# One index matmul for two parts of h: queries of tokens 64 to 255, and h's parts interleaved token by token

## The chip, the cores and the metric

The kernel runs on one core of a Trainium2 chip. The metric is the device time of one execution in microseconds (us); lower is better. TensorE (PE) multiplies, ScalarE (ACT), VectorE (DVE) and GpSimd (POOL) do the elementwise work, and SyncE (SP) issues all transfers, in order.

## The reference

One hybrid layer on x of 256 tokens by 4096. A vector c gives shift, scale and gate through w_ada (4096 x 12288); h, the modulated RMS norm of x, goes through one projection w_in, whose columns are split over a gated MLP, an attention and the attention's indexer.

```
mod = jax.nn.silu(c) @ w_ada + b_ada
shift, scale, gate = jnp.split(mod, 3, axis=-1)
h = rms_norm(x, norm_g) * (1 + scale) + shift          # (1, 256, 4096)
z = h @ w_in
uA, vA, gA, qB, kB, vB, gB, qI, kI, wI = jnp.split(z, offs, axis=-1)
yA = chunked_sgu(uA, vA, ...)
dots  = einsum('bqhd,bsd->bqhs', qI, kI)               # 32 index heads of 128
score = einsum('bqh,bqhs->bqs', wI, relu(dots))
score = where(causal, score, -inf)
_, sel = lax.top_k(score, 64)                          # 64 keys for each query
yB = attention of q over the selected keys and values, with a bias by distance
y  = concat([norm(yA) * silu(gA), norm(yB) * silu(gB)]) @ w_out
out = x + gate * y
```

A token t has t + 1 causal keys. For the tokens 0 to 63 these are at most 64, so top_k takes all of them whatever the scores are.

## The kernel before

All matmuls of the projections run in a 32-bit form with reduced precision (F32R), and float32 accuracy comes from splitting both operands in two: h = h_hi + h_lo, w = w_hi + w_lo, and the product is h_hi w_hi + h_lo w_hi + h_hi w_lo. h is the stationary operand (128 rows of the contraction by 128 tokens), w the moving one (up to 512 columns), so a pair of one contraction row block and one column group takes 3 parts x 2 token blocks = 6 matmuls.

A *tile* is two contraction row blocks of one column group. `stream` lists the tiles in order, and `step(t)` does for each: `load_w(t + 3)` (SP, into one of 4 raw buffers), `split(t)` (ACT makes whi; DVE and POOL share wlo = raw - whi by columns, POOL taking 352 of 512 on average in the early part), the adds of a visit that ended two tiles earlier (`add_to`: DVE adds PSUM to the group's sum, in the first block ACT copies), one `tick` of the work that runs beside, and `multiply(t)`, 12 matmuls. whi and wlo have 4 buffers each, two tiles' worth.

The contraction (32 row blocks) is cut into 8 *blocks* of 4, since h of a block needs shift and scale of its rows, and these come from 16.8 MB of w_ada a block. While block b is multiplied, `pace` spreads the ada work of the next block over the tiles, 33 steps a block: a transfer of 512 KB (SP, 2 buffers), and DVE's multiply-add into `acc` (L196). A buffer comes free when DVE is done with it, and SP issues the next ada transfer and the raw loads behind it in that order. `make_h` then sums `acc` over partitions on PE (L265), scales on ACT, and subtracts on POOL and DVE.

Each block visits 23 column groups, two tiles each: first the index columns (32 heads of 128 and the 160 columns kw of index keys and head weights, cut into two visits of 336 columns and seven of 512), then v and u of the MLP, then q, k, v of the attention. That makes 4 tiles of 336 columns and 42 of 512. In block 7 there are no ada steps of h left; `indexer` runs beside it: for each of 8 groups of 4 heads and each token block n, `turn` transposes the queries on PE with the flip matrix (L531), ACT copies them, `weigh` multiplies with the keys (L547), ACT takes relu, and DVE adds with the head's weight. After the 8 blocks come the gate columns (128 tiles, contraction whole) and w_out (128 tiles, y as the stationary operand), with attention, mixing and the gate's ada work beside.

Of the kernel before, what the change touches and what calls it, by code (L numbers as in the profile page):

```python
# [15 lines left out]
P = 128  # L16
# [26 lines left out]
def layer(ctx, tc, x, c, w_ada, b_ada, norm_g, w_in, ln_v_g, ln_v_b, w_s, b_s, q_norm_g,  # L43
# [213 lines left out]
    h_hi, h_lo = {}, {}  # L257
# [57 lines left out]
    def make_h(b, accs):  # L315
# [9 lines left out]
        hh = hp.tile([P, nk, 256], F32R, name=f"hh{k0}")  # L325
        hts, hl = [], None
        for j in range(0, nk, 2):
            modulate(b, md, j, hh[:, j:j + 2])
            yield
# [51 lines left out]
    def visit(src, parts, ks, c0, w, read, soon=False, before=None):  # L381
        v = dict(src=src, parts=parts, ks=ks, c0=c0, w=w, read=read, soon=soon, before=before)
# [36 lines left out]
    def multiply(t):  # L419
# [5 lines left out]
        (ah, al), w, n_k = v["parts"], v["w"], len(v["ks"])  # L425
        nk = len(hi)
        todo = [(part, kk, n) for kk in range(nk) for part in range(2) for n in range(NT)]
        todo += [(2, kk, n) for kk in range(nk) for n in range(NT)]
        if t + 1 == len(stream):
            todo.sort(key=lambda x: x[2])  # L430
        for part, kk, n in todo:
            k = v["ks"][i + kk]
            a = al if part == 1 else ah
            b = lo if part == 2 else hi
# [642 lines left out]
```

## Time and profile before

| | us |
|---|---|
| median of 3 runs | 1894.25 (1889.58 to 1897.37) |
| the profiled execution | 1888.63 |
| its span, first to last instruction | 1886.9 |
| first matmul with h | 70.3 |
| blocks 0 to 7 of the contraction | 70.3 to 1120.8 |
| gate columns and w_out | 1120.8 to 1886.9 |

Times in rows are us from the span's start unless marked ns. PE's busy time includes the modelled ends of pipelined matmuls, so the distance from one start to the next tells its pace. A block's bounds are the starts of its first matmul: 70.3, 202.6, 328.3, 455.6, 581.8, 709.2, 836.1, 961.4, and 1120.8 for the gate columns.

### The profile page before, as it was taken

What the parts mean: (1) busy time and instruction counts of PE and PEld (TensorE: products, weight loads), DVE (VectorE), ACT (ScalarE), POOL (GpSimd) and SP (SyncE); (2) the same over time, 40 slices, a digit from 0 to 9 for tenths busy, and PEclk for the clock granted to TensorE, in tenths of its full rate; (3) what the DMA queues carried; (4) which work ended last, traced back from release to release, by engine and by line L of the source; (5) the groups of instructions that cost most, each with busy time, mean ns of one, the idle gap of its engine ahead of it and who ended that gap; (6) DMA issues with size and microseconds to landing.
All of it is one profiled execution on the core that took longest, in us unless ns stands there. A gap on an engine that the chain in (4) does not pass through costs nothing. (4 is left out here: it accounts for less than half of the span.)

```text
span 1886.9 us, 27998 instructions
## 1 busy us (share of the span) xinstructions
PE 1824.8 (97%) x8324; PEld 1490.3 (79%) x8324; DVE 1447.4 (77%) x1762; ACT 933.8 (49%) x1737; POOL 1295.3 (69%) x1339
## 2 busy tenths in 40 slices
PE   5799999999999999999999999999999999999998
PEld 2487878878888888788888777787888888888887
DVE  4666888888888888888777898877777677677754
ACT  4356545344453454444445556566654554444443
POOL 0366777777777777777675546766567777877786
PEclk9899999999999999999999999999999999999999
DMA  9999998999989989999874477876789799899964
GB/s 311 339 338 340 332 322 304 331 316 306 335 304 322 321 300 324 328 309 340 284 207 146 128 224 262 272 257 202 242 281 312 248 323 338 295 307 350 334 212 156
DMA packets 269554, 542.58 MB, mean 288 GB/s; under 512 B 17270, under 2 KB 29784, under 8 KB 269404
## 3 DMA queue, kind: packets, MB, share of 16 engines
q1 hardware_dynamic: 269404, 540.79, 84.6%
q8 instruction: 68, 1.11, 0.2%
q14 instruction: 82, 0.67, 0.1%
HBM read 536.51 MB, written 4.22 MB: 287 GB/s over the span
## 5 line engine op out<-in xcount | busy, mean ns | idle before, releaser
L416 POOL TENSOR_TENSOR wlo<-raw,whi 128x512 fp32r<-128x512 f32 (+1 forms) x1248 | 1220.3, 1004 | 536.9 <-ACT whi L408 448.2
L408 ACT ACTIVATE whi<-raw 128x512 fp32r<-128x512 f32 (+1 forms) x1248 | 730.9, 619 | 834.9 <-DMA raw<-in_w_in_dram 407.5
L414 DVE TENSOR_TENSOR wlo<-raw,whi 128x320 fp32r<-128x320 f32 (+2 forms) x624 | 640.7, 1028 | 323.2 <-ACT whi L408 209.4
L435 PE MATMUL mm_ps<-whi,hh 128*128 128x512 f32 (+1 forms) x1984 | 620.4, 394 | 11.4 <-ACT whi L408 9.4
L435 PE MATMUL mm_ps<-whi,hl 128*128 128x512 f32 (+1 forms) x1984 | 604.9, 386 | 2.4 <-DVE hl L303 2.4
L435 PE MATMUL mm_ps<-wlo,hh 128*128 128x512 f32 (+1 forms) x1984 | 525.4, 386 | 5.7 <-DVE wlo L414 4.1
L196 DVE SCALAR_TENSOR_TENSOR acc<-wa,csil,acc 128x1024 f32<-128x1024 f32 x341 | 436.3, 1279 | 57.1 <-DMA wa<-in_w_ada_dram 56.4
L435 PEld LDWEIGHTS mm_ps<-wlo,hh 128*128 128x128 f32 x1984 | 368.9, 188 | 83.8 <-POOL wlo L416 8.8
L435 PEld LDWEIGHTS mm_ps<-whi,hh 128*128 128x128 f32 x1984 | 363.5, 189 | 90.2 <-ACT whi L408 19.9
L435 PEld LDWEIGHTS mm_ps<-whi,hl 128*128 128x128 f32 x1984 | 371.2, 188 | 77.3 <-DVE hl L303 2.9
L435 PE MATMUL mm_ps<-whi,yh 128*128 128x512 f32 x512 | 158.2, 390 | 0.0
L435 PE MATMUL mm_ps<-whi,yl 128*128 128x512 f32 x512 | 158.0, 389 | 0.0
L435 PE MATMUL mm_ps<-wlo,yh 128*128 128x512 f32 x512 | 137.5, 390 | 0.2
L435 PEld LDWEIGHTS mm_ps<-wlo,yh 128*128 128x128 f32 x512 | 95.9, 188 | 21.2 <-POOL wlo L416 1.5
L435 PEld LDWEIGHTS mm_ps<-whi,yh 128*128 128x128 f32 x512 | 95.9, 188 | 20.4 <-ACT whi L408 0.4
L435 PEld LDWEIGHTS mm_ps<-whi,yl 128*128 128x128 f32 x512 | 96.1, 188 | 20.0
L802 DVE TENSOR_TENSOR qi<-qi,mm_ps 128x512 f32<-128x512 f32 (+2 forms) x126 | 73.2, 616 | 0.0
L217 PE MATMUL acc<-wa,csil 128*1 128x512 f32 x64 | 28.1, 629 | 13.2 <-DMA wa<-in_w_ada_dram 13.2
L802 DVE TENSOR_TENSOR u<-u,mm_ps 128x512 f32<-128x512 f32 x56 | 35.6, 675 | 0.0
L802 DVE TENSOR_TENSOR v<-v,mm_ps 128x512 f32<-128x512 f32 x56 | 35.6, 675 | 0.0
L802 DVE TENSOR_TENSOR q<-q,mm_ps 128x512 f32<-128x512 f32 x56 | 35.6, 675 | 0.0
L222 DVE SCALAR_TENSOR_TENSOR accs<-wa,csil,accs 128x1024 f32<-128x1024 f32 x15 | 19.2, 1283 | 17.9 <-DMA wa<-in_w_ada_dram 17.8
(173 smaller groups left out, 797.2 us busy)
## 6 DMA issues: line engine op xcount, KB each, us to landing
raw<-in_w_in_dram SPq DMA_DIRECT2D x464, 512.0 KB, 5.9
wa<-in_w_ada_dram SPq DMA_DIRECT2D x384, 512.0 KB, 5.1
raw<-in_w_out_dram SPq DMA_DIRECT2D x128, 512.0 KB, 6.0
raw<-in_w_in_dram SPq DMA_DIRECT2D x32, 336.0 KB, 4.8
xs<-in_x_dram SPq DMA_DIRECT2D x8, 512.0 KB, 5.4
xres<-in_x_dram SPq DMA_DIRECT2D x8, 512.0 KB, 6.8
out_dram<-yt SPq DMA_DIRECT2D x16, 256.0 KB, 3.6
wk<-rb_d SPq DMA_DIRECT2D x16, 128.0 KB, 4.7
```

The lines of the kernel that those rows point to most:

```text
L196: nc.vector.scalar_tensor_tensor(dst, src, csil[:, k:k + 1], dst, op0=OP.mult, op1=OP.add)
L217: nc.tensor.matmul(acc[g:g + 1, s, :w], csil[:, k:k + 1], wt[:, s], start=i < 4, stop=i >= KC // 2 - 4)
L222: nc.vector.scalar_tensor_tensor(accs, wt, csil[:, k:k + 1], accs, op0=OP.mult, op1=OP.add)
L408: nc.scalar.activation(hi[kk][:, :w], raw[:, kk, :w], AF.Copy)
L414: nc.vector.tensor_sub(lo[kk][:, :cut], raw[:, kk, :cut], hi[kk][:, :cut].bitcast(F32))
L416: nc.gpsimd.tensor_sub(lo[kk][:, cut:w], raw[:, kk, cut:w], hi[kk][:, cut:w].bitcast(F32))
L435: nc.tensor.matmul(v["ps"][n][:, :w], a[k][:, n * P:(n + 1) * P], b[kk][:, :w], start=(i + kk == 0 and part == 0), stop=(i + kk == n_k - 1 ...
L802: nc.vector.tensor_add(z, z, p)
```

## The change

For the index queries, the first token block shrinks to the tokens 64 to 127, and the two parts of h of these 64 tokens stand side by side as one stationary operand of 128 columns (`packed`). One matmul with whi then gives h_hi w_hi in the even output rows and h_lo w_hi in the odd ones; one with wlo gives h_hi w_lo and, besides, h_lo w_lo. A packed pair takes 5 matmuls: that one twice, and the three parts of the second token block. The rows are summed where the indexer turns them: in place of four transposes, four matmuls with `fold`, a 128 x 64 matrix with two ones in each column. Scoring and choosing of the first token block then run on 64 queries; the mask of the tokens 0 to 63 is set to 0 and cut causally.

For that, h_hi and h_lo of a block are one tile hx, interleaved token by token. Each other matmul with h reads its stationary operand with a step of two elements. `make_h` scales once, copies to hx's even places and subtracts into its odd ones. kw becomes a visit of its own of 160 columns, and all eight index groups are 512 wide. The gate's steps and the mixes get a yield more each.

```diff
-        xT[b] = hp.tile([P, nk, 256], F32, name=f"xT{starts[b]}", tag=f"hl{starts[b]}")
+        xT[b] = (hp if b else zp).tile([P, nk, 256], F32, name=f"xT{starts[b]}", tag=f"hx{b}" if b else "v0")
...
+    def room_of_h(b):
+        return hp.tile([P, BLOCKS[b], 256, 2], F32R, name=f"hx{b}", tag=f"hx{b}")
+
+    def keep_h(b, hx):
         for j in range(BLOCKS[b]):
-            h_hi[starts[b] + j] = hh[:, j]
-            h_lo[starts[b] + j] = hl[:, j]
+            h_hi[starts[b] + j] = hx[:, j, :, 0]
+            h_lo[starts[b] + j] = hx[:, j, :, 1]
+            h_both[starts[b] + j] = hx[:, j, 64:128].rearrange("p a b -> p (a b)")
...
         for j in range(0, nk, 2):
-            modulate(b, md, j, hh[:, j:j + 2])
-            yield
             hts.append(s2.tile([P, 2, 256], F32, name="ht", tag="s2"))
             modulate(b, md, j, hts[-1])
             yield
+        hx = room_of_h(b)
         for j in range(0, nk, 2):
+            nc.scalar.activation(hx[:, j:j + 2, :, 0], hts[j // 2], AF.Copy)
+            yield
+            nc.gpsimd.tensor_sub(hx[:, j, :, 1], hts[j // 2][:, 0], hx[:, j, :, 0].bitcast(F32))
+            nc.vector.tensor_sub(hx[:, j + 1, :, 1], hts[j // 2][:, 1], hx[:, j + 1, :, 0].bitcast(F32))
...
+        for k, b in zip(ks, hi):
+            if v["packed"]:
+                todo += [(0, h_both[k], b), (1, half(ah, k, 1), b), (1, half(al, k, 1), b)]
+            else:
+                todo += [(n, half(a, k, n), b) for a in (ah, al) for n in range(NT)]
+        for k, b in zip(ks, lo):
+            todo += [(n, h_both[k] if v["packed"] and n == 0 else half(ah, k, n), b) for n in range(NT)]
...
-    early.append((O_KW - 176, 336, [("qi7", 336, 176), ("kw", 0, 160)]))
-    early.append((O_KW - 512, 336, [("qi7", 0, 336)]))
-    for g in range(7):
+    add_group("kw", O_KW, 160)
+    for g in range(8):
         add_group(f"qi{g}", O_QI + 512 * g, 512)
...
+            q = 64 * (n + 1)
             for hh in range(4):
-                nc.tensor.transpose(tp[:, hh * P:(hh + 1) * P], groups[f"qi{g}"][:, n, hh * P:(hh + 1) * P],
-                                    flip)
+                z = groups[f"qi{g}"][:, n, hh * P:(hh + 1) * P]
+                if n:
+                    nc.tensor.transpose(tp[:, hh * P:(hh + 1) * P], z, flip)
+                else:
+                    nc.tensor.matmul(tp[:, hh * q:(hh + 1) * q], z, fold, start=True, stop=True)
...
-    GATE_STEPS = 4 * 36
+    GATE_STEPS = 4 * 37
...
-        mixed = later(24, mixes(), 20)
+        mixed = later(28, mixes(), 21)
```

On PE at the head of block 1 (hh_1517 and hl_1637 are h_hi and h_lo of that block, 128x336 or 128x512 the output, x4 four in a row) the order before is this, two narrow tiles, and further on one full tile:

```order
L435 MATMUL mm_ps<-whi,hh_1517 128x336 x2
L435 MATMUL mm_ps<-whi,hl_1637 128x336 x2
L435 MATMUL mm_ps<-whi,hh_1517 128x336 x2
L435 MATMUL mm_ps<-whi,hl_1637 128x336 x2
L435 MATMUL mm_ps<-wlo,hh_1517 128x336 x4
L435 MATMUL mm_ps<-whi,hh_1517 128x336 x2
...
L435 MATMUL mm_ps<-whi,hh_1517 128x512 x2
L435 MATMUL mm_ps<-whi,hl_1637 128x512 x2
L435 MATMUL mm_ps<-whi,hh_1517 128x512 x2
L435 MATMUL mm_ps<-whi,hl_1637 128x512 x2
L435 MATMUL mm_ps<-wlo,hh_1517 128x512 x4
```

In the changed kernel the same place, the two kw tiles and the first index tile, has this (hx_1544 is the interleaved h of the block):

```order
L444 MATMUL mm_ps<-whi,hx_1544 128x160 x8
L444 MATMUL mm_ps<-wlo,hx_1544 128x160 x4
L444 MATMUL mm_ps<-whi,hx_1544 128x160 x8
L444 MATMUL mm_ps<-wlo,hx_1544 128x160 x4
L444 MATMUL mm_ps<-whi,hx_1544 128x512 x6
L444 MATMUL mm_ps<-wlo,hx_1544 128x512 x4
```

Four narrow tiles of 12 became two narrower ones, and each index tile behind them has 10 matmuls, three of whi and two of wlo for each contraction row block.

On ACT, near the end of block 0, where h of block 1 is made (xT_217 is the turned x of that block, q the sums of the attention's queries), before:

```order
L800 ACTIVATE q_183<-mm_ps 128x512 x2
L280 ACTIVATE hh_1517<-xT_217,md 128x256 x2
L408 ACTIVATE whi<-raw 128x512 x2
L280 ACTIVATE ht<-xT_217,md 128x256 x2
L408 ACTIVATE whi<-raw 128x512 x2
L800 ACTIVATE q_184<-mm_ps 128x512 x2
L280 ACTIVATE hh_1517<-xT_217,md 128x256 x2
L408 ACTIVATE whi<-raw 128x512 x2
L280 ACTIVATE ht<-xT_217,md 128x256 x2
L408 ACTIVATE whi<-raw 128x512 x2
```

And in the changed kernel:

```order
L819 ACTIVATE q_183<-mm_ps 128x512 x2
L280 ACTIVATE ht<-xT_217,md 128x256 x2
L410 ACTIVATE whi<-raw 128x512 x2
L280 ACTIVATE ht<-xT_217,md 128x256 x2
L410 ACTIVATE whi<-raw 128x512 x2
L819 ACTIVATE q_184<-mm_ps 128x512 x2
L336 ACTIVATE hx_1544<-ht 128x512
L410 ACTIVATE whi<-raw 128x512 x2
L336 ACTIVATE hx_1544<-ht 128x512
L410 ACTIVATE whi<-raw 128x512 x2
```

Four scalings into hh are gone, two copies of 512 into hx stand behind the scalings into ht, and the scalings start at the same step.

On PE in block 7, in the indexer, before and then in the changed kernel (flip turns the queries, ix holds the keys and scores, 128x128 or 128x64 is the output):

```order
L531 MATMUL ms_ps<-flip,qi_166 128x128 x4
L435 MATMUL mm_ps<-whi,hh_9195 128x512 x2
L435 MATMUL mm_ps<-whi,hl_9306 128x512 x2
L435 MATMUL mm_ps<-whi,hh_9195 128x512 x2
L435 MATMUL mm_ps<-whi,hl_9306 128x512 x2
L435 MATMUL mm_ps<-wlo,hh_9195 128x512 x4
L547 MATMUL ms_ps<-ix,qit 128x128 x4
```

```order
L444 MATMUL mm_ps<-wlo,hx_8994 128x512 x4
L546 MATMUL ms_ps<-fold,qi_168 128x64 x4
L444 MATMUL mm_ps<-whi,hx_8994 128x512 x6
L444 MATMUL mm_ps<-wlo,hx_8994 128x512 x4
L563 MATMUL ms_ps<-ix,qit 64x128 x4
L444 MATMUL mm_ps<-whi,hx_8994 128x512 x6
L444 MATMUL mm_ps<-wlo,hx_8994 128x512 x4
```

The turn of the first token block is four plain matmuls with 64 columns where four transposes with 128 stood; the four scoring matmuls behind it have 64 output rows and the same 128 columns.

## Rows read from the trace of the kernel before

**Rows 1.** The page: busy us, share of the span, instructions, by engine.

```profile
PE 1824.8 (97%) x8324; PEld 1490.3 (79%) x8324; DVE 1447.4 (77%) x1762; ACT 933.8 (49%) x1737; POOL 1295.3 (69%) x1339
```

**Rows 2.** Timeline, head of block 2: start, duration; PE, then ACT.

```profile
328.28 0.47 PE L435 MATMUL mm_ps<-whi,hh 128*128 128x336 f32 x2
...
330.12 0.47 PE L435 MATMUL mm_ps<-whi,hh 128*128 128x336 f32 x2
...
340.02 0.73 PE L435 MATMUL mm_ps<-whi,hh 128*128 128x512 f32 x2 [1.47 <-ACT whi L408]
...
342.88 0.62 PE L435 MATMUL mm_ps<-whi,hh 128*128 128x512 f32 x2
...
345.60 0.62 PE L435 MATMUL mm_ps<-whi,hh 128*128 128x512 f32 x2
...
327.18 0.93 ACT L408 ACTIVATE whi<-raw 128x336 fp32r<-128x336 f32 x2 [1.79 <-DMA raw<-in_w_in_dram]
...
339.33 1.15 ACT L408 ACTIVATE whi<-raw 128x512 fp32r<-128x512 f32 x2 [4.07 <-DMA raw<-in_w_in_dram]
```

**Rows 3.** Busy time by block: block 2, sum of 1 to 6, blocks 0 and 7.

```profile
core 0: us, PE busy (x) PEld busy (x) DVE busy (x) ACT busy (x) POOL busy (x), PEclk, DMA share, GB/s
...
328.30:455.60 127.30, 125.10 (x570) 103.22 (x569) 107.87 (x131) 56.95 (x101) 93.98 (x95) 1.00 0.92 315
...
sum 758.80, PE 749.29 PEld 620.59 DVE 639.15 ACT 342.81 POOL 562.96; mean PE 124.88 PEld 103.43 DVE 106.53 ACT 57.13 POOL 93.83
...
70.30:202.60 132.30, 128.32 (x568) 106.17 (x569) 88.83 (x95) 79.05 (x150) 90.36 (x93) 0.96 0.94 328
961.40:1120.80 159.40, 156.53 (x768) 129.83 (x768) 132.80 (x194) 85.24 (x139) 90.42 (x94) 1.00 0.56 169
```

**Rows 4.** Instructions in block 2 by shape: count | busy us, mean ns | idle before.

```profile
L414 DVE TENSOR_TENSOR wlo<-raw,whi 128x320 fp32r<-128x320 f32 x42 | 40.0, 954 | 15.4 <-ACT whi L408 13.8 <-PE mm_ps L435 1.3
L196 DVE SCALAR_TENSOR_TENSOR acc<-wa,csil,acc 128x1024 f32<-128x1024 f32 x31 | 39.7, 1279 | 3.4 <-DMA wa<-in_w_ada_dram 3.4
...
L802 DVE TENSOR_TENSOR qi<-qi,mm_ps 128x512 f32<-128x512 f32 x14 | 8.9, 674 | 0.0
...
L265 PE MATMUL ms_ps<-one,accs 128*128 128x1 f32 x16 | 1.8, 245 | 0.0
```

**Rows 5.** Waits in block 2: us in total, times, longest.

```profile
ACT whi L408 <- DMA raw<-in_w_in_dram: 54.6, 25, 4.1
...
ACT whi L408 <- PE mm_ps L435: 6.5, 7, 2.6
```

**Rows 6.** Waits of SP's queue in block 2.

```profile
SPq L178 <- DVE acc L196: 43.1, 23, 3.5
```

**Rows 7.** L408 alone behind the narrow tiles, blocks 1 and 6: busy (count).

```profile
216.00:232.00 16.00, 6.92 (x12) 1.00 0.96 329
...
849.00:865.00 16.00, 8.08 (x14) 1.00 0.97 345
```

**Rows 8.** Windows of 10 us in block 0.

```profile
100.00:110.00 10.00, 10.00 (x46) 8.29 (x45) 7.23 (x8) 6.71 (x13) 7.95 (x8) 1.00 0.98 350
110.00:120.00 10.00, 10.00 (x46) 8.29 (x45) 5.51 (x7) 5.31 (x11) 5.67 (x7) 1.00 1.00 348
```

**Rows 9.** DMA issues: count, size, us to landing.

```profile
raw<-in_w_in_dram SPq DMA_DIRECT2D x464, 512.0 KB, 5.9
wa<-in_w_ada_dram SPq DMA_DIRECT2D x384, 512.0 KB, 5.1
...
raw<-in_w_in_dram SPq DMA_DIRECT2D x32, 336.0 KB, 4.8
```

**Rows 10.** Timeline, block 7, PE around a turn.

```profile
989.44 0.70 PE L435 MATMUL mm_ps<-whi,hh 128*128 128x512 f32 x2
...
992.29 0.60 PE L531 MATMUL ms_ps<-flip,qi 128*128 128x128 f32 x4
992.64 0.71 PE L435 MATMUL mm_ps<-whi,hh 128*128 128x512 f32 x2
```

More of the change, by code (lines that the diff above doesn't have):

```diff
@@ L324, in make_h @@
         md = box[0]
[L325 to L326 removed]
+        hts = []
         for j in range(0, nk, 2):
[L328 to L329 removed]
             hts.append(s2.tile([P, 2, 256], F32, name="ht", tag="s2"))
@@ L379, in layer, with visit @@
     stream = []
-    def visit(src, parts, ks, c0, w, read, soon=False, before=None):
-        v = dict(src=src, parts=parts, ks=ks, c0=c0, w=w, read=read, soon=soon, before=before)
+    def visit(src, parts, ks, c0, w, read, packed=False, before=None):
+        v = dict(src=src, parts=parts, ks=ks, c0=c0, w=w, read=read, packed=packed, before=before)
         visits.append(v)
@@ L424, in multiply, with half @@
             v["ps"] = [mm.tile([P, 512], F32, name="mm_ps", tag="mm") for _ in range(NT)]
[L425 to L428, printed above, removed]
-        if t + 1 == len(stream):
[L430 to L434, printed above, removed]
-            nc.tensor.matmul(v["ps"][n][:, :w], a[k][:, n * P:(n + 1) * P], b[kk][:, :w],
-                             start=(i + kk == 0 and part == 0),
-                             stop=(i + kk == n_k - 1 and part == 2))
+        (ah, al), w, ks = v["parts"], v["w"], v["ks"][i:i + len(hi)]
+        def half(a, k, n):
+            return a[k][:, n * P:(n + 1) * P]
+        todo = []
+        for k, b in zip(ks, hi):
[5 more added lines that the diff above has]
+            todo += [(n, h_both[k] if v["packed"] and n == 0 else half(ah, k, n), b) for n in range(NT)]
+        if t + 1 == len(stream):
+            todo.sort(key=lambda x: x[0])
+        ends = {n: max(j for j, x in enumerate(todo) if x[0] == n) for n in range(NT)}
+        begun = set() if i == 0 else {0, 1}
+        for j, (n, a, b) in enumerate(todo):
+            nc.tensor.matmul(v["ps"][n][:, :w], a, b[:, :w], start=n not in begun,
+                             stop=i + len(hi) == len(v["ks"]) and j == ends[n])
+            begun.add(n)
     reads = []
@@ L444, in step @@
         del reads[:len(due)]
-        for v in due:
-            if v["soon"]:
-                v["read"](v["ps"])
         split(t)
@@ L450, in step @@
         for v in due:
-            if not v["soon"]:
-                v["read"](v["ps"])
+            v["read"](v["ps"])
         v, i = stream[t]
@@ L515, in indexer @@
         wi = small([P, NT, IDX_HEADS], "wi")
+        fold = cp.tile([P, 64], F32, name="fold")
+        nc.vector.memset(fold, 0.0)
+        for r in range(2):
+            nc.gpsimd.affine_select(fold, fold, pattern=[[2, 64]], compare_op=OP.not_equal, fill=1.0,
+                                    base=-126 - r, channel_multiplier=1)
         tp = misc()
@@ L808, in layer @@
             visit(w_in_t, (h_hi, h_lo), list(range(starts[b], starts[b] + nk)), c0, w, add_to(parts, b == 0),
-                  soon=0 < b and nk == 2)
+                  packed=parts[0][0].startswith("qi"))
     n_early = len(stream)
```

51 lines of the change are left out of this document (25 added, 26 removed).

## The prediction

> **What bounds the kernel now.** I read the page first. TensorE (PE) is busy 97% of the span, VectorE 77% [rows 1]. A busy PE is not yet a PE at its pace, so I looked for the pace next. In the timeline a full tile of w_in (12 matmuls of 512 columns) begins 2.72 us after the one before (342.88 to 345.60), 0.2267 us a matmul; a 336-column tile takes 1.84 us (328.28 to 330.12), 0.153 a matmul [rows 2]. The two differ by 176 columns and 73 ns, so streaming costs 0.417 ns a column and each matmul 13 ns beside it.
>
> A block is 46 tiles, 42 full and 4 narrow: 42 x 2.72 + 4 x 1.84 = 121.6 us. Once a block PE also sums the modulations (L265, 16 records, 1.8 us [rows 4]), which makes 123.4. The trace's blocks 1 to 6 take 758.8 / 6 = 126.5 us on average [rows 3]. So 3.1 us a block are stalls, although PE is shown busy for 124.9 of the 126.5. One stall is visible: the first full tiles after the four narrow ones. Tile 5 starts at 340.02, after 1.47 us on ACT's whi, and ACT had itself waited 4.07 us for a transfer; five tiles before, ACT had begun its split 2.9 us before PE needed it (327.18 against 330.12) [rows 2]. So in the six middle blocks PE is the bound, and the supply of split weights is only just behind it.
>
> That supply I read from three views. In a typical block ACT waits 54.6 us for raw tiles, and 6.5 us for PE to free its buffers [rows 5]. SP, which issues every transfer in order, waits 43.1 us for VectorE to free an ada buffer, and the next raw load stands behind that wait [rows 6]. DMA share is 0.92 in block 2, and windows of 10 us with a share of 0.98 and 1.00 move 350 and 348 GB/s where that block moves 315, so the transfers are close to their end too [rows 3, 8]. Right after the narrow tiles, where ACT is behind and nothing downstream holds it, it does 12 to 14 half tiles in 16 us (the two ends shown; over six such windows 12, 12, 12, 13, 13 and 14, in all 76 in 96 us): 2.53 us a tile, with ends 2.67 and 2.29 [rows 7]. **The supply can therefore give a tile every 2.53 us, where PE takes one every 2.72.** VectorE alone says the same: 0.70 ada steps a tile x 1.279 + 0.954 + 0.674 = 2.52 us [rows 4].
>
> **What the change removes.** A packed tile has 10 matmuls and not 12: 10 x 0.2267 = 2.27 us. Per block, the 8 index groups are now 16 packed tiles; kw is 2 tiles of 160 columns where 4 tiles of 336 stood. A 160-column matmul streams in 67 + 13 = 80 ns, and the nearest row for its weight load is L265, whose moving operand is a single column: 1.8 / 16 = 0.1125 us a pair of load and matmul [rows 4]. I take that: 12 x 0.1125 = 1.35 us a tile (0.96 if only the stream counted; 0.8 us a block between the two). PE's work in a block becomes 2 x 1.35 + 16 x 2.27 + 28 x 2.72 + 1.8 = 117.0 us. That is 6.4 less than 123.4.
>
> **What it doesn't remove.** Bytes: 32 ada loads and 42 raw loads of 512 KB with 4 of 336 KB are 39,232 KB a block; 32 and 44 of 512 with 2 of 160 are the same 39,232 KB [rows 9], 40.17 MB. Splits and adds keep their columns too. So in the packed zone PE wants a tile every 2.27 us from a supply that gives 2.53. Zone one, 18 tiles (kw and index): PE 2.7 + 36.3 = 39.0; supply 18 x 2.53 = 45.5, less the 2.9 us lead with which a block begins, 42.6. PE stalls 3.6 us. Zone two, 28 tiles: PE 76.2 + 1.8 = 78.0; supply 70.8, so PE bounds again and the lead grows back. I leave it half of today's 3.1 us of stalls, since the other half follows the narrow tiles. Block: 42.6 + 78.0 + 1.5 = 122.1, a gain of **4.4 us in each of blocks 1 to 6**. With 2.67 a tile it is 48.1 - 2.9 + 78.0 + 3.1 = 126.3, a gain of 0.2; with 2.29 the first zone's stall goes and 6.4 is the end. I take the middle pace, because it is the mean of six blocks.
>
> Block 0 is another matter. Its loads run faster (0.94 share and 328 GB/s over the whole, start included [rows 3]), and the two windows at share 0.98 and 1.00 lie in its index tiles [rows 8]. There is nothing to feed them faster: I take 1 us, between 0 and 6.4.
>
> Block 7 has a DMA share of 0.56 [rows 3], so PE's 6.4 us arrive. Against them stands the indexer, which runs there. Its first-token-block turn was 4 transposes, 0.48 us in a tile (3.20 from 989.44 to 992.64, less 2.72 [rows 10]). Now it is 4 plain float32 matmuls with fold, and a plain one shows as two records (L265: 16 for the 8 of a block), so 8 x 0.1125 = 0.90. Eight groups: 8 x 0.42 = 3.4 us more. Net gain 3.0 us (6.4 if the new form cost what the transposes do). Scoring keeps its matmul count and columns: 0.
>
> **Costed at nothing.** From 1120.8 to the end the work stays but for extra yields; 0. Making h: two copies replace four of eight scalings on ACT, busy 57.1 of 126.5 us a block [rows 3], and the last subtractions still stand three to four tiles ahead of their use, some 8 us of cover; were that gone, a copy and a subtraction, 1 to 2 us a block.
>
> **The stationary operand with step 2.** All unpacked matmuls with h, and the second token block of packed ones, now load every second float32. No load in the trace does. Ends: 0.1125 us as today, hidden under the 0.213 us stream, or twice that, 0.225, which is 12 ns over it. It touches 28 x 12 x 8 + 6 x 16 x 8 + 128 x 12 = 4992 wide matmuls: 0 or 58 us. I take 0, as even most of a doubling stays covered. The Trainium skill (SBUF — State Buffer, Specifications) says that SBUF is read in 16-byte lines and that two hits a line keep full bandwidth; a step of 8 bytes leaves two, so by it the price is 0 and the sum stands, and by the doubling it is 58 us worse; no row shows which.
>
> **Sum.** 6 x 4.4 + 1 + 3.0 = 30.4 us off the profiled execution: 1888.6 - 30.4 = 1858.2. That execution was 5.6 us under the median of the three runs, so against 1894.25 I say **1864 us**.
>
> **Rivals.**
> *The whole saving arrives.* If the queue never idled, 40.17 MB at 348 GB/s would take 115.4 us a block, under PE's 117.0. For it: those windows. Against it: block 2's share of 0.92, and SP's waits in order. It gives 8 x 6.4 - 3.4 = 47.8, so 1846. The Trainium skill (DMA: Bandwidth & Descriptors, Specifications) has about 358 GB/s for a core's share of HBM; that is near what the windows show, and by it, as an estimate, a block's bytes would take 112 us and this rival would hold.
> *The supply decides.* If 2.67 is what it sustains, the six blocks give 0.2 each, block 0 nothing, block 7 3.0: 4 us, 1890, no measurable change. For it: ACT's 54.6 us on transfers. Against: half of the six windows are quicker.
> *The strided load shows.* It decides once a load lasts over 0.213 us; at 0.219 (30.4 / 4992 = 6 ns) the gain is eaten, and at the doubling the time is 1864 + 58 = 1922.
>
> **Chances.** Forecast, 1850 to 1884: 0.65. Whole saving 0.13, supply 0.12, strided load 0.10. This measurement tells about 0.5%, 9.5 us, from nothing; so faster 0.78, same 0.12, slower 0.10. The range 1846 to 1890 holds the first three up to their own points and leaves out the slow one and what lies beyond the ends.
>
> **What would show it.** Packed tiles that start 2.27 us apart at the head of zone one and some 2.5 apart later, PE waiting on whi there with ACT waiting on raw; full tiles at 2.72 still; blocks 1 to 6 near 122 us; DMA share 0.95 or more in them; block 7 near 156; fold matmuls at 0.9 us a group. Wrong if wide matmuls with step-2 operands stand over 0.227 us apart (strided load), if blocks are near 118 (whole saving), or if packed tiles come 2.7 apart from the start (supply).

## The result and the profile after

The change made the kernel slower: 1907.05 us in the median (1898.22 to 1912.54, 12 runs) against 1892.89 (1887.4 to 1901.17, 12 runs) of the kernel before beside it, a ratio of 1.0071 (95% interval 1.0052 to 1.009). The prediction was 1864, with a range from 1846 to 1890. The profiled execution took 1898.22 us, the fastest of the 12, its span is 1896.5; so what follows accounts for the 9.6 us between the two profiled spans, and not for all of the 14.2 between the medians.

The first row of the page, which answers to [rows 1], and two groups of its weight loads (xcount | busy us, mean ns | idle before):

```profile
PE 1828.8 (96%) x8100; PEld 1473.7 (78%) x8100; DVE 1445.1 (76%) x1749; ACT 932.4 (49%) x1721; POOL 1307.2 (69%) x1342
...
L444 PEld LDWEIGHTS mm_ps<-whi,hx 128*128 128x128 f32 x3712 | 704.8, 195 | 172.7 <-ACT whi L410 33.2
...
L444 PEld LDWEIGHTS mm_ps<-whi,yh 128*128 128x128 f32 x512 | 96.0, 188 | 20.1 <-ACT whi L410 0.2
```

224 instructions fewer on PE, and yet 4.0 us more of busy time: what was saved in number came back in length. A weight load of hx, nearly all of them with step 2, lasts 195 ns on average, one of neighbouring elements (yh, in w_out) 188.

Busy time by block as in [rows 3]: block 2, then the sum over blocks 1 to 6; after that blocks 0 and 7 and the gate columns of branch B, and last the same columns before:

```profile
329.88:457.80 127.92, 124.01 (x537) 99.39 (x536) 106.36 (x131) 56.02 (x99) 93.34 (x95) 1.00 0.92 314
...
sum 765.69, PE 744.95 PEld 597.13 DVE 633.73 ACT 339.95 POOL 565.75; mean PE 124.16 PEld 99.52 DVE 105.62 ACT 56.66 POOL 94.29
```

```profile
69.50:200.84 131.34, 127.03 (x536) 103.24 (x537) 85.51 (x95) 78.34 (x147) 90.70 (x94) 0.96 0.95 334
966.53:1123.60 157.07, 156.62 (x765) 129.84 (x764) 129.45 (x193) 84.36 (x140) 96.12 (x96) 1.00 0.56 171
...
1346.70:1538.90 192.20, 190.32 (x856) 158.74 (x855) 141.38 (x148) 103.37 (x190) 129.48 (x136) 1.00 0.80 271
```
```profile
1342.10:1529.70 187.60, 185.54 (x857) 154.13 (x856) 138.91 (x149) 102.08 (x189) 128.71 (x136) 1.00 0.83 278
```

Against [rows 3] blocks 1 to 6 are 6.9 us longer in all, block 0 is 1.0 and block 7 is 2.3 shorter. The gate columns of branch B lose 4.6, those of A 1.8 (221.3 before, 223.1 after). That makes 10.0; with some 0.5 given back ahead of block 0 and in w_out it is the 9.6 us between the spans.

To see where in a block it goes, I cut blocks 1 to 6 into the index zone (18 tiles in both kernels, with the same bytes) and the second zone (28 tiles). The sums of the index zones, before and then after, and of the second zones, before and then after:

```profile
sum 283.59, PE 277.50 PEld 232.60 DVE 244.43 ACT 117.54 POOL 208.72; mean PE 46.25 PEld 38.77 DVE 40.74 ACT 19.59 POOL 34.79
```
```profile
sum 280.43, PE 259.93 PEld 194.75 DVE 233.57 ACT 118.66 POOL 206.76; mean PE 43.32 PEld 32.46 DVE 38.93 ACT 19.78 POOL 34.46
```
```profile
sum 475.22, PE 471.80 PEld 387.99 DVE 394.68 ACT 225.23 POOL 354.25; mean PE 78.63 PEld 64.67 DVE 65.78 ACT 37.54 POOL 59.04
```
```profile
sum 485.26, PE 485.02 PEld 402.38 DVE 400.15 ACT 221.29 POOL 358.99; mean PE 80.84 PEld 67.06 DVE 66.69 ACT 36.88 POOL 59.83
```

The index zone, which was to shrink to 42.6 us, took 46.7 (280.43 / 6), and before it had taken 47.3: packing gave 0.5 us a block there. The second zone, which is not packed, became 1.7 us longer. PE's timeline of the changed kernel in block 2 (start, duration) says why, first the kw tiles, then packed tiles, then a full tile and the sum of modulations behind it:

```profile
329.88 1.06 PE L444 MATMUL mm_ps<-whi,hx 128*128 128x160 f32 x8
...
331.25 1.11 PE L444 MATMUL mm_ps<-whi,hx 128*128 128x160 f32 x8
...
336.21 1.66 PE L444 MATMUL mm_ps<-whi,hx 128*128 128x512 f32 x6 [1.03 <-ACT whi L410]
...
338.97 1.56 PE L444 MATMUL mm_ps<-whi,hx 128*128 128x512 f32 x6
...
341.29 1.55 PE L444 MATMUL mm_ps<-whi,hx 128*128 128x512 f32 x6
...
422.11 2.03 PE L444 MATMUL mm_ps<-whi,hx 128*128 128x512 f32 x8
...
424.91 1.84 PE L265 MATMUL ms_ps<-one,accs 128*128 128x1 f32 x16
```

A kw tile is 1.37 us and a packed tile 2.32 when it is fed, both near the prediction's 1.35 and 2.27. A full tile is 2.80 (422.11 to 424.91) where [rows 2] have 2.72: 0.2333 us a matmul, 6.7 ns more. The step-2 load shows, and in the packed zone PE waits for whi. SP's queue over blocks 1 to 6 (us in total, times, longest) points to who is behind that, after and then before:

```profile
SPq L178 <- DVE acc L196: 297.4, 146, 4.3
```
```profile
SPq L178 <- DVE acc L196: 272.8, 138, 3.9
```

### The profile page after: what moved, and what is told of

It reads as the page before. It is cut to its first block, busy times and chain, and to the rows that moved or that the text cites. A ratio compares the mean times of both kernels' runs of the same rounds, so it can differ in the third digit from the quotient of the medians.

```text
span 1896.5 us, 27521 instructions
## 1 busy us (share of the span) xinstructions
PE 1828.8 (96%) x8100; PEld 1473.7 (78%) x8100; DVE 1445.1 (76%) x1749; ACT 932.4 (49%) x1721; POOL 1307.2 (69%) x1342
## 4 chain that ended last, share of the span: by engine, by line
PE 75%; DMA 12%; DVE 5%; issue 3%; POOL 3%; ACT 1%; SPq 0%; POOLq 0%; ACTq 0%; DVEq 0%
PE mm_ps L444 70%; DMA raw<-in_w_in_dram 8%; DMA wa<-in_w_ada_dram 4%; POOL wlo L418 2%; DVE acc L196 1%; DVE wlo L416 1%; PE ms_ps L563 1%; ACT whi L410 1%; PE ms_ps L265 1%; PE ms_ps L704 1%; PE x_ps L236 0%; DVE qi L821 0%; PE ms_ps L903 0%; PE ms_ps L546 0%; DMA xs<-in_x_dram 0%
## 5 line engine op out<-in xcount | busy, mean ns | idle before, releaser
L444 PE MATMUL mm_ps<-whi,hx 128*128 128x512 f32 (+1 forms) x3712 | 954.7, 397 | 21.0 <-ACT whi L410 19.1
L444 PEld LDWEIGHTS mm_ps<-whi,hx 128*128 128x128 f32 x3712 | 704.8, 195 | 172.7 <-ACT whi L410 33.2
L444 PE MATMUL mm_ps<-wlo,hx 128*128 128x512 f32 (+1 forms) x1984 | 551.8, 395 | 8.6 <-DVE wlo L416 4.7
L444 PEld LDWEIGHTS mm_ps<-wlo,hx 128*128 128x128 f32 x1984 | 375.7, 195 | 106.9 <-POOL wlo L418 27.8
L821 DVE TENSOR_TENSOR qi<-qi,mm_ps 128x512 f32<-128x512 f32 x112 | 71.3, 675 | 0.0
L575 DVE SCALAR_TENSOR_TENSOR ix<-rel,wi,ix 64x128 f32<-64x128 f32 (+1 forms) x62 | 28.7, 463 | 3.6 <-ACT rel L568 0.9
```

Source lines behind the costliest of these rows:

```text
L444: nc.tensor.matmul(v["ps"][n][:, :w], a, b[:, :w], start=n not in begun, stop=i + len(hi) == len(v["ks"]) and j == ends[n])
L575: nc.vector.scalar_tensor_tensor(sc, r[:q, a * S:(a + 1) * S], ws, sc, op0=OP.mult, op1=OP.add)
L821: nc.vector.tensor_add(z, z, p)
```

## The experiments

Two theories stood after this. T1: each step-2 read costs 6.7 ns. T2: the index zone is held by its supply and not by PE, so that packing can't show there. Each ratio below is to the kernel before, run beside it, with its 95% interval. The block times are those of one profiled execution each; where blocks wait for their supply, they differ by up to 6 us within a run, in the run with another pace by 11.

**The step and the packing, one at a time.** The first run reads neighbouring elements (hence other values), the second keeps the step for the first token block alone, the third takes packing out, the fourth takes out both.

In the first and the fourth:

```diff
-            h_hi[starts[b] + j] = hx[:, j, :, 0]
-            h_lo[starts[b] + j] = hx[:, j, :, 1]
+            row = hx[:, j].rearrange("p a b -> p (a b)")
+            h_hi[starts[b] + j] = row[:, 0:256]
+            h_lo[starts[b] + j] = row[:, 256:512]
```

In the second, where a part is now the pair of its two token blocks:

```diff
+    def of(hx, j, part):
+        return hx[:, j, part:256:2], hx[:, j, 256 + P * part:256 + P * (part + 1)]
...
-            h_hi[starts[b] + j] = hx[:, j, :, 0]
+            h_hi[starts[b] + j] = of(hx, j, 0)
```

In the third and the fourth:

```diff
-                  packed=parts[0][0].startswith("qi"))
+                  packed=False)
```

> The changed kernel, but each matmul with h reads 128 neighbouring elements of the interleaved tile instead of every second one (the operands hold other values than they should, so the output is not the reference's; all work and its order stay). Theory, the step-2 read costs about 6.7 ns in each wide matmul: it shows wherever TensorE bounds, that is 28 tiles x 12 x 8 in the second zone and 128 x 12 in the gates, 28 us, while in the index zone of blocks 0 to 6 it hides behind the transfers: 1907 - 28 = about 1878 us, ratio to the kernel before 0.992, wide matmuls 0.227 us apart again, gate columns A near 213 us instead of 223. Rival, the slow-down comes from the other edits (more instructions in making h, fold, yields): 1907 us again, ratio 1.007, tiles at 2.80 us.

> The changed kernel with only the first token block of h interleaved; the second block's two parts lie apart, each contiguous. Output as in the reference. Of 4992 wide matmuls that read with a step, 28 x 6 x 8 + 128 x 6 = 2112 are left, none in packed tiles. Theory, a fixed price of about 6.7 ns a read: half of the 28 us comes back, 1907 - 14 = 1893 us, ratio 1.000, and within a tile the matmuls of token block 0 stand 0.233 apart, those of token block 1 0.227. Rival, the price hangs on something else than each read: 1907 us (1.007) or all of it back, 1878 (0.992).

> The changed kernel with the packed matmuls taken out: index tiles have 12 matmuls again, all with step 2 (values of the index queries in the first token block are then summed wrongly by fold; all other work stays). TensorE's work in a block becomes 44 x 12 x 0.2333 + 2 x 1.37 + 1.8 = 127.7 us, which then bounds everywhere. Theory, packing saved little because the index zone waits for transfers and not for TensorE: blocks 1 to 6 near 129, 1.4 us more than with packing, block 7 7 us more, in all 1907 + 8 + 7 + 2 = about 1924 us, ratio 1.016. Rival, packing gave its 7.4 us a block and something else lost them: 1907 + 59 = 1966, ratio 1.039.

> Both at once: contiguous reads (as in the kernel with those alone) and no packing; the output is not the reference's. TensorE's work in a block 44 x 2.72 + 2.7 + 1.8 = 124.2 us, some 126 with stalls as before the change. Theory: the kernel before, with fold's 3.4 us in block 7 and small edits: 1893 + 3 = 1896, ratio 1.002; so packing alone, read against the run with contiguous reads and packing (about 1878), is worth some 18 us, of which 7 in block 7 and about 1.5 in each other block, where the sum of the prediction had 4.4. Rival, packing alone is worth what the prediction said, 30 us or more: then contiguous reads with packing must end at 1865 or less, ratio 0.985.

Measured: 1.0032 (1.0016 to 1.0048), 1.0051 (1.0031 to 1.0071), 1.0154 (1.0134 to 1.0173) and 1.0064 (1.004 to 1.0088); in us 1897.33, 1898.63, 1919.32 and 1902.93. Full tiles of the run with contiguous reads, by PE's timeline:

```profile
547.59 1.98 PE L445 MATMUL mm_ps<-whi,hx 128*128 128x512 f32 x8
...
550.31 1.99 PE L445 MATMUL mm_ps<-whi,hx 128*128 128x512 f32 x8
```

2.72 us again. In the second run, with half the steps, a full tile lasts from 545.01 to 547.78, 2.77 us, between 2.72 and 2.80, and in the second zone of its block 2 half of the weight loads last 194 ns and half 187. So T1's price is right, and it goes by the read. But of the 28 us that I had expected back from it only 7 came (1.0071 to 1.0032). And the blocks' sum:

```profile
sum 762.18, PE 733.38 PEld 579.00 DVE 637.50 ACT 336.78 POOL 564.72; mean PE 122.23 PEld 96.50 DVE 106.25 ACT 56.13 POOL 94.12
```

That is 127.0 a block with TensorE work of 117.0. Without packing, in the fourth run, it is the same:

```profile
sum 762.28, PE 753.11 PEld 620.05 DVE 635.52 ACT 337.88 POOL 561.45; mean PE 125.52 PEld 103.34 DVE 105.92 ACT 56.31 POOL 93.58
```

So T2 holds beyond the index zone: over blocks 1 to 6 the six matmuls in a pair or the five make no difference in these two executions, and most of the 0.3% between the two runs is block 7 (160.3 and 164.7). In the third run, where the step lifts PE's work to 127.7, blocks are 128.9 (773.2 / 6), and PE bounds.

**What holds a block: bytes or VectorE.** Both with contiguous reads. The first lets two ada steps share one load, the second cuts VectorE's step to 64 columns; the modulations are then other values.

```diff
+            if ns == 2 and k0 % 2:
+                ada_tiles.append(shared[-1])
+                return
...
+                    w = 64 if ns == 2 else 1024
-                    nc.vector.scalar_tensor_tensor(dst, src, csil[:, k:k + 1], dst,
+                    nc.vector.scalar_tensor_tensor(dst[:, :w], src[:, :w], csil[:, k:k + 1], dst[:, :w],
```

> The kernel with contiguous reads, and in blocks 0 to 6 two ada steps share one transfer of 512 KB (so 16 loads a block and not 32, and shift and scale are not the reference's; VectorE's work, PE's and all else stay). Theory, the index zone is held by bytes: its 18 tiles carry 12.1 MB and not 15.4, 37 us at 330 GB/s, under TensorE's 39: the zone falls from 46 or 47 us to 39 to 41, blocks to 118 to 120, the time from 1897 to about 1850. Rival, VectorE's 2.52 us a tile holds it (SP's waits are for VectorE's acc): zone 46 or 47, time 1897.

> The kernel with contiguous reads, and in blocks 0 to 6 VectorE's ada step takes 64 columns in place of 1024 (shift and scale are not the reference's; all transfers stay, VectorE gives buffers free about 1.1 us sooner and loses some 36 us of work a block). Theory, bytes hold the index zone: 46 us as before, blocks 125 to 127, time 1890 to 1897, and SP's waits for acc become waits for the transfers themselves. Rival, VectorE holds it: zone 39 to 41, blocks 118 to 120, time about 1850.

Measured, in two runs each: 0.9651 (0.9619 to 0.9682), 1825.29 us, and 0.9809 (0.9777 to 0.984), 1855.13 us. Blocks 1 to 6 of the first and of the second:

```profile
sum 705.44, PE 704.59 PEld 584.46 DVE 620.29 ACT 357.59 POOL 570.70; mean PE 117.43 PEld 97.41 DVE 103.38 ACT 59.60 POOL 95.12
```
```profile
sum 728.36, PE 719.84 PEld 577.43 DVE 508.47 ACT 344.65 POOL 572.80; mean PE 119.97 PEld 96.24 DVE 84.75 ACT 57.44 POOL 95.47
```

Either one alone helps, so neither bytes nor VectorE alone is the answer: blocks of 117.6 with half the bytes, so TensorE's 117.0 was right, and of 121.4 with all bytes and a short step. What bytes and VectorE have in common is SP: it issues the next ada load only when VectorE has freed a buffer, and raw loads stand behind it.

**A copy of the packed operand, and another pace.** The first keeps h's parts apart and contiguous and gives the packed operand 2 KB a partition of its own; the second also moves ada steps to the second zone.

```diff
+            pair = hp.tile([P, 4, 64, 2], F32R, name=f"pair{b}", tag=f"hb{b + 1}")
+            nc.scalar.activation(pair[:, :, :, 0], hx[0][:, :, 64:P].bitcast(F32), AF.Copy)
+            nc.gpsimd.tensor_copy(pair[:, :, :, 1], hx[1][:, :, 64:P].bitcast(F32))
...
+    share = [0.6 if v["packed"] else 1.0 for v, i in stream]
```

> Output as in the reference. Packing kept, but h's two parts lie apart and contiguous in blocks 0 to 6, and the packed operand (64 tokens of h_hi and h_lo, interleaved, 2 KB a partition) is a small copy of its own in the room that block b + 1 will fill later; two more small copies a block on ACT and GpSimd. Only block 7 keeps the interleaved first token block. Step-2 reads fall from 4992 to 264. Theory, as the run with contiguous reads: blocks 126 to 127 since transfers hold the index zone, gate columns B back near 188 from 192, time 1893 to 1897, ratio 1.001 to 1.003. Rival, the run with contiguous reads was slow for its odd values: then 1880 or less, ratio 0.994.

> The kernel with the small copy of the packed operand, and an ada pace that counts a packed tile as 0.6 of another: about 9.7 ada steps of a block in its 18 index tiles and 23.3 in the 28 others, where 12.9 and 20.1 stood. Output as in the reference. Theory, the index zone is held by its bytes and the second zone has room: 13.8 MB at 330 GB/s are 41.8 us in place of 46 or 47, and the second zone's 26.9 MB at 335 are 80.2, blocks 122, time 1895 - 7 x 4.7 = about 1862, ratio 0.985. Rival, the second zone moves no more than its 310 GB/s (its loads stand behind VectorE in SP's order): 26.9 MB take 86.8, blocks 128, time 1900, ratio 1.005.

Measured: 1.0037 (1.002 to 1.0054), 1898.2 us, as the run with contiguous reads; 1.0107 (1.008 to 1.0134), 1911.42 us, slower still. Blocks 1 to 6 of the first, and SP's wait in them:

```profile
sum 771.51, PE 737.35 PEld 574.89 DVE 635.64 ACT 338.16 POOL 563.91; mean PE 122.89 PEld 95.82 DVE 105.94 ACT 56.36 POOL 93.98
```
```profile
SPq L178 <- DVE acc L196: 290.6, 141, 5.3
```

The blocks of the second are 129.5 on average (776.80 / 6). Its index zones, with 9.5 ada steps where the first has 12.8, take 46.8 us against 47.5 (280.88 and 284.72 / 6), and its second zones 1.5 us more. So bytes in the index zone, T2 as I had it, are not the cause either.

**Taking the order apart.** w_in tiles issued by ACT (with the copy of the operand, in the kernel before, and in the changed kernel), and more of wlo on GpSimd. With ACT's queue the issue also moves from the head of a step to behind the split:

```diff
-        nc.sync.dma_start(raw[:, :, :w], v["src"][:, v["ks"][i]:v["ks"][i] + nk, c0:c0 + w])
+        eng = nc.scalar if AHEAD <= t < at[-1] else nc.sync
+        eng.dma_start(raw[:, :, :w], v["src"][:, v["ks"][i]:v["ks"][i] + nk, c0:c0 + w])
...
-        load_w(t + AHEAD)
...
         split(t)
+        load_w(t + AHEAD)
...
-    POOL_EARLY, POOL_REST = 352, 288
+    POOL_EARLY, POOL_REST = 400, 288
```

> The kernel with the small copy of the packed operand, and in blocks 0 to 6 the w_in tiles are issued from ACT's queue, right behind ACT's split of the tile before, so that SP has ada loads alone and a raw load no longer stands behind SP's wait for VectorE's acc. All loads, their sizes and all arithmetic stay. Theory, halving the ada bytes gave 9 us a block and freeing VectorE 5.5, because two things hold a block: 40.2 MB, which alone take 121 us, and SP's order, in which a wait for VectorE stops the raw loads, which makes it 127. Without that order the blocks come to 121 to 123, DMA share 0.96 or more: 1897 - 7 x 5 = about 1862 us, ratio 0.985. Rival, it is VectorE's own time (its 2.5 us a tile, with ada data late or not) and not the order: blocks 126 to 128, ratio 1.003.

> The kernel before, with the w_in tiles of blocks 0 to 6 issued from ACT's queue in the same way. TensorE has 123.4 us of work in each of its blocks, so that no more than 126.5 - 124 = 2 to 3 us a block can come: about 1877 us, ratio 0.991. Read against the packed kernel with the same queues, it says what packing is worth once loads don't stand behind VectorE: theory 15 us or so, rival nothing.

> The changed kernel as it is, with the w_in tiles of blocks 0 to 6 issued from ACT's queue. TensorE has 117.0 + 6.5 ns x (28 x 12 + 16 x 6) = 119.8 us a block. Theory: blocks 122 to 124, 1907 - 7 x 4.5 = about 1875, ratio 0.991, and some 10 us more than the kernel with the copy, 4.5 of it in gate columns B. Rival, as it was: 1907, ratio 1.007.

> The kernel with the small copy of the packed operand, queues as they were, and GpSimd takes 800 of a tile's 1024 columns of wlo in blocks 0 to 6, where it took 704; VectorE's share falls from 320 to 224 columns, 0.954 to about 0.68 us a tile, 0.27 x 46 = 12.6 us less of its work in a block. Theory, VectorE frees the ada buffers sooner and SP stands less: freeing 36 us gave 5.5, so some 2 us a block, 1897 - 14 = about 1883, ratio 0.996. Rival, GpSimd's 2.0 us a tile becomes 2.3 and its wlo is the late one: no gain or a loss, ratio 1.003 or more.

> Output as in the reference: the kernel with the small copy of the packed operand, w_in tiles from ACT's queue in blocks 0 to 6, and GpSimd's share of wlo at 800 of 1024 columns. Each alone gave 0.5% and 0.2% against the kernel with the copy. Theory, both lighten what stands before a load and add up: 1898 - 11 - 4 = about 1883 us, ratio 0.996. Rival, with the raw loads off SP VectorE's share no longer matters: as the run with ACT's queue alone, 0.9985.

Measured, in that order: 0.9985 (0.9972 to 0.9998), 1.0021 (1.0003 to 1.0038), 1.0083 (1.006 to 1.0106), 1.0019 (1.0001 to 1.0037), and both together 0.9988 (0.9963 to 1.0012). The first four miss their theories by far, the last came out as its rival said. Where ACT's queue was used, block 0 grew, by 2 to 9 us; in the kernel before it went from 132.3 to 139.3, which takes back what blocks 1 to 6 gave there (753.4 for 758.8). In the first run blocks 1 to 6 are still 126.2 (757.34 / 6), and the wait has moved: VectorE now waits for its ada data, over blocks 1 to 6, 97.2 us where the kernel with the copy and one queue shows 24.7.

```profile
DVE acc L196 <- DMA wa<-in_w_ada_dram: 97.2, 69, 4.3
```

The ada load itself still starts only when its buffer is freed, and now it is the late one. I read this so: the raw loads that stood behind SP's wait were one half of the matter, and the other is that an ada load is asked for too late. The next runs test it.

**A third ada buffer.** Room was made by letting u3 fall on u2 (another output). With loads two steps ahead, the buffer of a new load was freed one step earlier; with three ahead, SP waits as it always did, and only the depth grows. The third run asks whether packing pays where the supply is fast: half the ada bytes, contiguous reads, no packing.

```diff
-            wt = wp.tile([P, per, ns, width], F32, name="wa", tag="wa", bufs=2)
+            wt = wp.tile([P, per, ns, width], F32, name="wa", tag="wa", bufs=3)
...
     load_ada()
     load_ada()
+    load_ada()            # the second run alone
```

> The kernel with the small copy of the packed operand and a third ada buffer (room made by letting the fourth u group fall on the third, so the output is not the reference's, and by one buffer less in the later stages, whose times are not read). Loads are issued two steps ahead as before, so the buffer of a new ada load was freed a whole step earlier and SP has no wait for VectorE. Theory, SP's wait in order is what lifts a block from 121 to 127: blocks 1 to 6 at 121 to 123, DMA share 0.96, SP's waits for acc gone. Rival, bytes: blocks at 126 or 127 all the same, share 0.92.

> The same with three ada loads ahead: SP waits for VectorE's step as in the kernel before, but a load has one step more to land. Theory of SP's order: blocks 126 to 128, SP's waits for acc near 20 us in an index zone. Rival, the depth of the loads (a load takes 5.2 us to land, and two buffers are one too few): blocks 121 to 123 here, and not in the run with two ahead.

> Contiguous reads, half the ada bytes, no packing (values not the reference's): against the run with half the ada bytes and packing, whose blocks took 117.6 us on average. Theory, with a faster supply TensorE's work shows in full: 44 x 2.72 + 2.7 + 1.8 = 124.2, blocks 124.5 to 125, time 1825 + 8 x 7.2 = about 1883. Rival, packing is worth little even then: blocks 118 to 121, time below 1855.

Measured: 0.9636 (0.9596 to 0.9676), 1823.08 us, in two runs; 0.9974 (0.9955 to 0.9994), 1886.5; 0.9929 (0.9903 to 0.9955), 1878.12. Blocks 1 to 6 of the first, and SP's waits in them; then the same wait of the second:

```profile
311.34:429.32 117.98, 117.19 (x537) 97.50 (x536) 104.98 (x129) 58.98 (x100) 95.23 (x96) 1.00 0.96 340
...
sum 704.92, PE 703.88 PEld 584.65 DVE 627.55 ACT 353.70 POOL 571.62; mean PE 117.31 PEld 97.44 DVE 104.59 ACT 58.95 POOL 95.27
```
```profile
SPq L426 <- DVE wlo L444: 298.4, 234, 3.8
...
SPq L178 <- DVE acc L196: 51.6, 67, 2.3
```
```profile
SPq L178 <- DVE acc L196: 336.4, 142, 4.8
```

Same bytes, same steps of VectorE, same queue: 117.5 a block instead of 126 to 129, and what went is the wait for acc, some 50 us where the kernels with two buffers and one queue have 270 to 300. What SP waits for now are raw buffers (L426): it is ahead of its consumers. The blocks of the second and the third run:

```profile
sum 761.71, PE 730.06 PEld 575.44 DVE 641.38 ACT 338.64 POOL 567.12; mean PE 121.68 PEld 95.91 DVE 106.90 ACT 56.44 POOL 94.52
```
```profile
sum 745.24, PE 745.24 PEld 621.52 DVE 636.98 ACT 364.31 POOL 579.59; mean PE 124.21 PEld 103.59 DVE 106.16 ACT 60.72 POOL 96.60
```

With the wait kept, depth gives little: 127.0 a block against 128.6 in the kernel with the copy, 0.6% of the time (0.9974 against 1.0037). And without packing the blocks of the third run are 124.2, against 117.6 with it.

**The same in the whole computation.** acc's copy moves into the room of the h that it makes, and every third ada load takes the buffer that it leaves.

```diff
-            accs = t4.tile([P, 2, 512], F32, name="accs", tag="t4")
+            accs = hp.tile([P, 2, 512], F32, name="accs", tag=f"hb{b}")
...
+            third = ns == 2 and len(ada_loads) % 3 == 0
+            wt = (t4 if third else wp).tile([P, per, ns, width], F32, name="wa", tag="t4" if third else "wa",
+                                            bufs=5 if third else 2)
```

> Output as in the reference: the kernel with the small copy of the packed operand; every third ada load of h goes to the fifth buffer of the pool that holds u, and acc's copy moves from there into the room of the h that it makes. Loads stay two steps ahead, so the buffer of each was freed a step earlier. Theory: blocks 117 to 118 as in the run that left the fourth u group out, later stages as before, 1823 to 1828 us, ratio 0.965. Rival, the copy of acc or the fifth buffer makes a wait of its own at the end of each block: a few us a block, 1840 or more, ratio 0.973.

> The kernel before with the same third ada buffer and no packing. TensorE has 123.4 us of work a block and no more to lose than its stalls: blocks 123.5 to 124, 1892 - 7 x 3 = about 1871 us, ratio 0.989. So packing would be worth 45 us or so in the company of the third buffer, where alone it was worth nothing. Rival, the buffer is what gives nearly all: 1840 or less, ratio below 0.973.

Measured: **0.9648 (0.9633 to 0.9664), 1827.14 us**, and 0.9866 (0.9853 to 0.988), 1867.25 us. Sum of the index zones and of the second zones of the first, and of the blocks of the second:

```profile
313.05:353.73 40.68, 39.80 (x185) 32.40 (x184) 39.28 (x48) 19.62 (x34) 35.15 (x36) 1.00 1.02 372
...
sum 237.92, PE 235.77 PEld 195.47 DVE 227.95 ACT 119.71 POOL 208.73; mean PE 39.29 PEld 32.58 DVE 37.99 ACT 19.95 POOL 34.79
```
```profile
sum 468.04, PE 468.04 PEld 389.16 DVE 400.78 ACT 233.77 POOL 362.20; mean PE 78.01 PEld 64.86 DVE 66.80 ACT 38.96 POOL 60.37
```
```profile
sum 740.88, PE 740.88 PEld 622.61 DVE 636.70 ACT 368.03 POOL 575.58; mean PE 123.48 PEld 103.77 DVE 106.12 ACT 61.34 POOL 95.93
```

With the third buffer PE is busy through every block, but for 0.4 us in an index zone. The third buffer alone is worth 1.3%, and packing, worth nothing or less without it, is worth another 40 us with it; in blocks 1 to 6 that is 5.8 us a block (123.5 less 117.7), of the 6.4 by which PE's work fell.

## Why the prediction was wrong

**PE's work was read rightly.** 123.4 us a block before and 117.0 after, from start-to-start distances: with the third buffer, and h read without the step, the runs show 123.5 and 117.7. The second zone was to be 78.0 and is 78.01 there. kw tile and packed tile came as said; fold adds 0.8 to 1.0 us to a tile where 0.90 stood. Block 7 (157.1 for 156) came out partly by luck: its 432 reads with step 2 cost 2.9 us that stood at 0, and PE's idle time there fell by 2.4 (159.40 less 156.53 busy [rows 3], then 157.07 less 156.62).

**The supply was not.** Between the profiled executions 30.4 us less was forecast and 9.6 more came, 40 apart. Some 25 of these lie in the index zones of blocks 1 to 6 (46.7 us for 42.6, six times), 8 in their second zones (80.9 for 78.0 + 1.5), 6 in the gate columns. The step that failed first is "18 x 2.53 = 45.5, less the 2.9 us lead, 42.6", and in it the pace of the supply. ACT's splits in block 4 of the changed kernel, of the first kw tile and of the first tile of the second zone, and then PE's start of the same two tiles, show both terms:

```profile
580.57 0.34 ACT L410 ACTIVATE whi<-raw 128x160 fp32r<-128x160 f32 x1 [1.25 <-POOL wlo L418]
...
630.22 1.16 ACT L410 ACTIVATE whi<-raw 128x512 fp32r<-128x512 f32 x2 [1.44 <-DMA raw<-in_w_in_dram]
```
```profile
585.03 1.06 PE L444 MATMUL mm_ps<-whi,hx 128*128 128x160 f32 x8
...
632.08 2.02 PE L444 MATMUL mm_ps<-whi,hx 128*128 128x512 f32 x8
```

ACT was 4.46 us ahead of PE at the head of the zone and 1.86 at its end, so the lead was there and most of the forecast 2.9 was spent. But the 18 splits took 49.65 us. Over blocks 1 to 6 they took 49.0 on average, 2.72 a tile (2.70 over the packed tiles alone), and the lead fell from 4.2 to 2.0. So the supply gave a tile every 2.7 us, near the rival's 2.67, and not every 2.53. I took 16-us windows behind the narrow tiles, where DMA share was 0.96 and 0.97 [rows 7], as a pace that lasts. The kernel before takes 47.3 us for the same tiles and bytes, where PE's own work is 45.4 (4 x 1.84 + 14 x 2.72); that row could not have told the supply's pace, but it would have said that PE already waited there.

I also read the wait of SP [rows 6] and the share of 0.92 [rows 3] as two signs of transfers near their end. They were one thing: the wait made the share. At 372 GB/s in an index zone, with all bytes, the transfers were not at their end at 350 [rows 8]. VectorE's 2.52 us a tile [rows 4], which seemed to say the same, adds up records that overlap. In block 2 of the run with the third buffer and packing (start, duration):

```profile
324.06 1.28 DVE L198 SCALAR_TENSOR_TENSOR acc<-wa,csil,acc 128x1024 f32<-128x1024 f32 x1
325.25 0.84 DVE L446 TENSOR_TENSOR wlo<-raw,whi 128x320 fp32r<-128x320 f32 x1
```

The second begins 0.09 us before the first ends. The index zones of that run go at 237.92 / 6 / 18 = 2.20 us a tile with the same steps of VectorE, which is busy for 37.99 of 39.65 us there: little of its time is left. Block 0, where the prediction saw nothing to feed its loads faster, gained the 1 us that it had; in that run it takes 121.9 us and not 131.3, so there too its loads could come faster.

So the rival *the supply decides* came true in its pace, by another mechanism than "2.67 is what it sustains": an ada load waits for the step that VectorE has just been given, and raw loads wait behind it. That PE had only 3.1 us of stalls a block hid that it was bound twice, by 123.4 of its own work and by a supply just as slow.

**The step-2 load was priced at 0** and costs 6.7 ns, "both ends" 0 and 12 ns. The reason that I gave, that the weight load hides under the stream, is refuted: the records of the load grew by 7 ns, far from the stream's 213, and the distance grew as much. The Trainium skill's rule (SBUF — State Buffer, Specifications (TRN2): full bandwidth needs two hits in a 16-byte line) would give 0, and this trace disagrees. Times 4992 it is 33 us of PE's work, which is what the rival *the strided load shows* priced; in time it cost 7 us (1.0071 against 1.0032 with contiguous reads), since blocks 1 to 6 were held by the supply. It shows nearly whole in the gate columns of branch B: 64 x 12 x 6.7 ns = 5.1, measured 4.6. In those of A, where PE was idle for 7.9 us before (221.30 less 213.45 busy), 1.8 came through. With this price a second zone comes to 78.0 + 28 x 12 x 6.7 ns = 80.3, and 80.9 was measured. Two rivals, the supply and the step, came true together, which no chance in the prediction covered.

**Not settled:** with packing and without the step the kernel is still 0.3% or 0.4% slower than before (first run, copy of the operand). Their blocks 1 to 6 are 0.5 and 2.1 us longer than before (127.0 and 771.51 / 6 = 128.6 against 126.5), each in one profiled execution. Stalls that lower the clock (below) and the copies in make_h are candidates; no run takes them apart. The clock would do by its size: its mean over all runs is 0.991 and 0.992 where the kernel before beside them has 0.996 and 0.995. As an estimate, time x (1 - clock) is 17 and 16 us against 8 and 9, so 9 and 7 us more if PE was busy throughout, and 6 and 7 us are to be explained. But the profiled execution of the kernel with the copy, at 0.995, took 1900.92 us where its median is 1898.2, so the clock alone it is not.

## What to carry to other kernels

Before pricing a saving on one engine, cut the kernel before into the stretches that the change will shorten, and ask of each stretch, whole, whether it already waits for its supply: here one row said 47.3, 1.9 more than PE's own work, where I forecast 42.6. A pace that is to carry a forecast is taken over the whole stretch, not behind its fastest part. A DMA share below 1 beside a long wait of the issuing queue was here not bandwidth at its end. Ask whose buffer the queue waits for: here a load that was issued one step after its buffer came free hardly held up the others. An operand's layout belongs in the price of every instruction that reads it, not only of those for which it was made.

## What the runs showed of the hardware

A stationary operand of float32 with a step of two elements costs 6.7 ns in each matmul of 512 columns (2.80 us a tile of 12 against 2.72), though its load of 195 ns, against 188, lies beside a stream of 213.

DMA of the one core that runs the kernel reached 372 GB/s over an index zone of 41 us in the run with the third buffer and packing, and 392 in another zone of that run:

```profile
549.35:588.29 38.94, 38.94 (x185) 32.71 (x184) 37.74 (x49) 20.65 (x36) 35.91 (x36) 1.00 1.04 392
```

The Trainium skill (HBM Reference, Specifications (TRN2)) says that a core that streams alone gets well above its share of 358; the trace agrees, so the 358 beside the prediction's first rival is no end for this kernel.

A stall of PE cost more than itself. In block 4 of the run with half the steps, the row of PE's timeline behind a stall, and windows of 2 us around it (length, then PE, PEld, DVE, ACT and POOL busy, granted clock, DMA share, GB/s):

```profile
616.16 1.92 PE L455 MATMUL mm_ps<-whi,hx 128*128 128x512 f32 x4 [2.34 <-ACT whi L421]
```
```profile
612.00:614.00 2.00, 1.73 (x7) 0.81 (x5) 0.96 (x2) 0.00 (x0) 0.62 (x2) 1.00 1.04 373
614.00:616.00 2.00, 0.00 (x0) 0.00 (x0) 1.29 (x1) 0.53 (x1) 0.00 (x0) 1.00 0.90 273
616.00:618.00 2.00, 1.84 (x5) 1.46 (x6) 1.34 (x2) 1.77 (x4) 1.82 (x2) 0.59 1.00 340
618.00:620.00 2.00, 2.00 (x7) 1.57 (x6) 2.00 (x4) 0.57 (x2) 2.00 (x3) 0.56 1.03 379
620.00:622.00 2.00, 2.00 (x11) 1.65 (x10) 2.00 (x3) 0.58 (x2) 2.00 (x3) 1.00 0.93 355
```

After 2.34 us without work the granted clock was 0.59 and 0.56 for two windows, so mostly its lower level of 1.2 GHz, and PE began 5 and 7 matmuls where 11 follow at full clock. In the kernel before the clock was 1.00 in all six index zones, in the changed kernel 0.97 and 0.96 in two of them.
